# Moving three pieces of work in a four-layer decoder trunk: the bias-table copies, the first memory loads, and the rotary query product

## The chip, the core and the metric

The kernel runs on one core of a Trainium2 chip. The metric is the device time of one execution in microseconds (us), the median over the runs shown. One more execution was taken with the hardware profiler, and all rows of the profile come from that one.

## The reference, cut to what matters

There are 256 rows of 2048 features, four layers and one memory of 256 rows that every layer attends to.

```python
mem_n = rmsnorm(mem, mem_norm)
for i in range(4):
    h = rmsnorm(x, norm_in[i])
    # kinds 0, 1, 2, 0: latent attention, sparse attention, window attention, latent attention
    self_out, mq, gate = branch[i % 3](h, w_in[i], ...)
    mem_out = memory_attention(mq, mem_n @ w_mem_kv[i])     # 4 heads of 256, softmax over the memory
    y = concat([self_out, mem_out]) * silu(gate)            # 2048 + 1024 features
    x = x + y @ w_out[i]
out = rmsnorm(x, final_norm)
```

- Latent attention (layers 0 and 3) projects h to a query vector of 1536, a key-value vector of 512 and one shared rotary key of 64. Each of its 16 heads then takes a query of 128 plain and 64 rotary features from the normalized 1536 (`w_uq`), and a key and a value of 128 from the normalized 512 (`w_ukv`).
- Sparse attention (layer 1) has 32 heads, 4 key heads, and 16 index heads: for each query it adds relu(index query · index key) over the 16 heads with weights, and only the 64 keys with the best sums count. A bias by distance and head is added to the logits.
- Window attention (layer 2) has the same heads, a window of 128, a sink for each head, and the same bias.

All is float32 at the input and the output.

## The kernel before, in words

**Products.** Each float32 operand is split into a high and a low part (`split`, L62: a copy on ScalarE makes the high part, a subtraction on VectorE the low one), and each product is made of high×high, high×low and low×high. `rows_by` (L212) puts 128 rows of x on the output partitions: for each tile of 128 features it makes 3 products for each of the two row tiles (L227 to L229), as wide as the columns asked for, 512 at most. `columns_by` (L232) puts the output columns on the partitions (L246, 512 wide, and L250, 256 wide). Weights come by `stage` (L190) through SyncE's DMA queue into `wr`, a ring of 5 buffers of 4 KB a partition; `parts_of` splits a tile of them into `wh` and `wl`, rings of 3. The sums stand in PSUM tiles `acc`, 4 in all. Smaller products and transposes use 4 PSUM tiles `mp`.

**Buffers by name.** `PQ` = 5 buffers hold queries and keys (`qn`, `kn`, `qS`, `mkr`, `mqT`), `AUX` = 3 hold values and the like (`va`, `qrT`, `vs`, `mvr`). A pool hands out its buffers in the order in which the code asks for them. `big0` to `big3` hold what lives through a layer: in layers 1 and 2 first `iqT` (the index queries) and then `vz` (the split values) in `big1` and `big2`. The ring `e` of 4 holds softmax rows, and in `select` the relu'd scores `rl`.

**Order.** A scheduler with a timeline model of the engines puts the instructions of each engine into one fixed queue when the kernel is built; what is wrapped in `tc.keep_in_program_order` keeps its place in its engine's queue. On the chip each queue runs in that order, and an instruction that has to wait holds all behind it.

**Stages.** `memory()` (L305) first makes the keys and values of the memory for all four layers, from `w_mem_kv`, and stores them to DRAM (`mkT`, `mv`) by GpSimd's DMA queue. The same loop makes two small bias tables (`bias_table`, 32×384), and spreads them by `table_copies` (L130) over 128 rows: 8 DMAs of 1.5 MB from DRAM to DRAM, one in each of its 8 steps, but two in step 1 and none in step 7.

Each layer then runs `first()`. For latent attention that is the "small projection" of 576 columns in two products of 288 (`kva`, `kvb`), which gives the key-value vector and the rotary key `kr`, and then 1536 columns `cq`. For the others it is `kv`, giving the doubled keys `kd` (`mixer.k`), then in layer 1 `select()`: index products `iq`, then for each block of 128 queries 16 small products `isp` (L745), each followed by a relu on ScalarE (`rl`, L748) and a weighted sum on VectorE (`sco`, L753), and then 8 rounds of MAX8 and MATCH_REPLACE8 on VectorE (L760, L761). After that, `vz` is zeroed by two memsets on GpSimd (L689) and filled.

Then come six parts in the order 4, 0, 1, 2, 3, 5: parts 4 and 5 are halves of the memory attention (`memory_project`, `memory_attend`), the others groups of self heads (`project`, `attend`). The output product `w_out` (L827) of a part runs after the next part's attention: 4 chunks of 512 columns, each added to x (L832).

`memory_project` (L476) asks for two value buffers `mvr` and a key buffer `mkr` for each of its two heads, and loads them by GpSimd's DMA queue; between, it makes the memory queries (`acc_mq`) and drains each into `mqT` by `head_parts` (L260: ScalarE copies, VectorE `zl` L265 and `mqT` L266). The scores `msp` (L502) need `mkr`.

`Latent.project` (L605) makes for its group of four heads first the rotary queries (`acc_qr`, `rows_by`, 256 columns, 12 feature tiles), turns and transposes them, then the plain queries `qn`, the keys `kn`, the values `va` and the gate.

Of the kernel before, what the change touches and what calls it, by code (L numbers as in the profile page):

```python
# [8 lines left out]
F32 = mybir.dt.float32  # L9
# [6 lines left out]
P = 128  # L16
S = 256
# [7 lines left out]
MEMW = 1024  # L25
ST = 2
N_TAB = 384
PQ, AUX, WR = 5, 3, 5


@with_exitstack
def kernel(ctx: ExitStack, tc: tile.TileContext, a: dict, out: bass.AP,
# [97 lines left out]
    def table_copies(v, g):  # L130
        src = bass.AP(tensor=flat[v].tensor, offset=flat[v].offset + g * 8 * N_TAB,
                      ap=[[0, P], [1, 8 * N_TAB]])
        tc.keep_in_program_order(nc.gpsimd.dma_start(tabs[v][g].rearrange("p h n -> p (h n)"), src))


    def rsqrt_mean(dst, ssq, n):
# [168 lines left out]
    def memory():  # L305
        mrstd = cst.tile([P, 2], F32, name="mrstd")
        m16 = cst.tile([P, 2], F32, name="m16")
        mbc = act.tile([P, S], F32, name="mbc", tag="kr", bufs=1)
        mss = small("mss", 8, bufs=2)
        mT = [act.tile([P, 2, 4, S], F32R, name="mT", tag=f"big{c}") for c in range(4)]  # L310

        def prepare(c):
            if c < 3:
                mft.append(features(a["l_mem"], c + 1))
            if c == 1:
                tc.keep_in_program_order(nc.sync.dma_start(ident, a["c_ident"]))
                nc.vector.tensor_copy(identr, ident)
            weighted_parts(mT[c], mft[c], c * 4)

        def memory_rows(c):  # L320
            q = act.tile([P, 2, 512], F32, name="mrow", tag="pq", bufs=PQ)
            for t in range(2):
                tc.keep_in_program_order(
                    nc.sync.dma_start(q[:, t, :], min_[t][:, c * 512:(c + 1) * 512]))
            return q

        def row_scales(mrow):
            for c in range(4):
                for t in range(2):
                    square_sum(mss[:, t * 4 + c:t * 4 + c + 1], mrow[c][:, t, :])  # L330
            s2 = small("ms2", 2)
            nc.vector.tensor_reduce(s2, mss.rearrange("p (t c) -> p t c", t=2), AX.X, OP.add)
            rsqrt_mean(mrstd, s2, D)
            nc.vector.tensor_scalar(m16, mrstd, 0.0625, None, op0=OP.mult)
            spread(mbc, m16)

        def values(i, p_, acc):
            v = [act.tile([P, 2, 512], F32R, name="mv", tag="aux", bufs=AUX) for z in range(2)]
            for t in range(2):
                sc = mrstd[:, t:t + 1]  # L340
                copy_act(v[0][:, t, :], acc[t], scale=sc)
                nc.vector.scalar_tensor_tensor(v[1][:, t, :], acc[t], sc, f32(v[0])[:, t, :],
                                               op0=OP.mult, op1=OP.subtract)
            for z in range(2):
                nc.gpsimd.dma_start(mv[i][p_][:, z], v[z])

        def keys(i, h, acc):
            kT = act.tile([P, 2, 2, S], F32R, name="mkT", tag="pq", bufs=PQ)
            for j in range(2):
                z = total(acc[j])  # L350
                zs = wk.tile([P, S], F32, name="zs", tag="z", bufs=3)
                nc.vector.tensor_mul(zs, z, mbc)
                split(kT[:, 0, j, :], kT[:, 1, j, :], zs)
            nc.gpsimd.dma_start(mkT[i][h], kT)

        copies = [(v, g) for v in range(2) for g in range(4)]
        for i in range(depth):
            w = a["w_mem_kv"][i]
            for p_ in range(2):

                begins = i == p_ == 0
                acc = rows_by(mT, 16, w, 0, (MEMW + p_ * 512, 512), "mv", prepare if begins else None)
                if begins:
                    mrow = [memory_rows(c) for c in range(4)]
                else:
                    values(i, p_, acc)
                for h in (2 * p_, 2 * p_ + 1):
                    acck = columns_by(mT, 16, w, 0, (h * 256, 256), "mk")
                    if begins and h == 0:
                        row_scales(mrow)  # L370
                        values(i, p_, acc)
                    keys(i, h, acck)
                if begins:
                    late_constants()
                step = 2 * i + p_
                if step == 0:
                    bias_table(0)
                    bias_table(1)
                if 2 <= step < 6:
                    first_rows(step - 2)  # L380
                    nm.chunk(step - 2)
                if step == 6:
                    nm.finish()
                for c in copies[:2 if step == 1 else 1]:
                    table_copies(*c)
                copies = copies[2 if step == 1 else 1:]


    def transposed(dst, srcs):
# [83 lines left out]
        return weights_T(es, [(0, 0), (1, 0), (1, 1)])  # L473


    def memory_project(nm, i, w, mq0, g0, part):  # L476
        kT, qT = [], []
        v = [act.tile([P, 2, 512], F32R, name="mvr", tag="aux", bufs=AUX) for z in range(2)]
        for z in range(2):
            nc.gpsimd.dma_start(v[z], mv[i][part][:, z])  # L480
        for h in range(2):
            k = act.tile([P, 2, 2, S], F32R, name="mkr", tag="pq", bufs=PQ)
            nc.gpsimd.dma_start(k, mkT[i][2 * part + h])
            kT.append(k)
            acc = columns_by(nm.at, 16, w, 0, (mq0 + part * 512 + h * 256, 256), "mq")
            q = act.tile([P, 2, 2, S], F32R, name="mqT", tag="pq", bufs=PQ)
            head_parts(q, acc)
            qT.append(q)
        return nm, kT, v, qT, gate(nm, w, g0 + 2048 + part * 512)
# [49 lines left out]
    class Latent:  # L539
# [6 lines left out]
        def first(self):  # L546
# [55 lines left out]
            for z, sg in zip(self.scale, (1.0, -1.0)):  # L602
                nc.vector.tensor_scalar(z, qr, sg * (A_NOPE + A_ROPE) ** -0.5, None, op0=OP.mult)

        def project(self, g):  # L605

            j = self.j
            wq, wkv = a["w_uq"][j], a["w_ukv"][j]
            qn, kn = [], []
            qr = act.tile([P, 4, S], F32R, name="qrT", tag="aux", bufs=AUX)  # L610
            v = act.tile([P, 2, 512], F32, name="va", tag="aux", bufs=AUX)
            acc = rows_by(self.cT[:3], 12, wq, 0, (g * 768, 4, 192, A_NOPE, A_ROPE), "qr")
            for t in range(2):
                rr = wk.tile([P, 4, A_ROPE], F32, name="qrr", tag="z", bufs=3)
                rope(rr, acc[t][:, :S].rearrange("p (h d) -> p h d", h=4), t, 4)
                rs = wk.tile([P, 4, 2, A_ROPE], F32R, name="qrs", tag="qrs", bufs=1)
                split(rs[:, :, 0, :], rs[:, :, 1, :], rr)
                transposed(lambda i0, i1: qr[:, i0:i1, t * P:(t + 1) * P],
                           [rs[:, h].rearrange("p a b -> p (a b)") for h in range(4)])
            for half in range(2):  # L620
                acc = columns_by(self.cT[:3], 12, wq, 0, (g * 768 + half * 384, 2, 192, 0, A_NOPE), "qn")
                q = act.tile([P, 2, 2, S], F32R, name="qn", tag="pq", bufs=PQ)
                head_parts(q, acc)
                qn.append(q)
            for half in range(2):
                acc = columns_by(self.cT[3:], 4, wkv, 0, (g * 1024 + half * 512, 2, 256, 0, A_NOPE), "kn")
                k = act.tile([P, 2, 2, S], F32R, name="kn", tag="pq", bufs=PQ)
                head_parts(k, acc)
                kn.append(k)
            acc = rows_by(self.cT[3:], 4, wkv, 0, (g * 1024, 4, 256, A_NOPE, A_NOPE), "va")  # L630
            for t in range(2):
                copy_act(v[:, t, :], acc[t])
            return qn, qr, kn, v, gate(self.nm, self.w, self.g0 + g * 512)

        def attend(self, qn, qr, kn, v, gT):
            y = act.tile([P, 2, 4, S], F32R, name="y", tag="y", bufs=2)
# [180 lines left out]

    nm = Norm(0)
    memory()

    for i in range(depth):
        kind = kinds[i]
# [4 lines left out]
        def w_out(part, y, last):  # L827
            for c in range(4):
                acc = rows_by([y], 4, a["w_out"][i], part * 4, (c * 512, 512), "wo")
                for t in range(2):  # L830
                    xs = x[t][:, c * 512:(c + 1) * 512]
                    nc.vector.tensor_add(xs, xs, acc[t])  # L832
                if last and nxt is not None:
                    nxt.chunk(c)
                if last and nxt is None:
# [8 lines left out]
        order = [4, 0, 1, 2, 3, 5]  # L844
        for n_, part in enumerate(order):
            if part >= 4:
                y = memory_attend(*memory_project(nm, i, mixer.w, mixer.mq0, mixer.g0, part - 4))
            else:
                y = mixer.attend(*mixer.project(part))
            if pending is not None:  # L850
                w_out(*pending, False)
            pending = (part, y)
# [86 lines left out]
```

## Time and profile before

| | us |
|---|---|
| runs | 2639.67, 2634.15, 2635.05 |
| median | 2635.05 |
| profiled execution, its own time | 2636.8 |
| span of the profiled execution | 2634.7 |
| TensorE busy in the span | 2601.2 (99%) |
| VectorE / ScalarE / GpSimd busy | 1884.1 / 1628.8 / 57.3 |

The span runs from the first to the last instruction in the trace. Busy times of the engines overlap. In rows of instructions the columns are: start in us, time in us, engine, source line, operation, output and inputs, their sizes, how many were merged into the row, and in brackets how long the engine had been idle before it and what ended that. Products on TensorE are pipelined: the time from the start of one to the start of the next is what one costs, and it is shorter than the time in its own row. In tables by stretch there stand start and end, the length, then for each engine its busy time and in brackets its instructions, then the granted TensorE clock (`PEclk`, 1.00 is full), the busy share of the DMA engines, and GB/s.

### The profile page before, as it was taken

How to read it: one execution, taken by the hardware profiler on the slowest of the kernel's cores; microseconds unless marked ns; L12 is line 12 of the kernel's file. 1: busy time of each engine (PE TensorE's matmuls, PEld its weight loads, DVE VectorE, ACT ScalarE, POOL GpSimd, SP SyncE). 2: the span in 40 equal slices, each digit the busy share in tenths (PEclk: the TensorE clock that was granted, in tenths of full speed). 3: DMA queues.
4: the chain of work that ended last, by engine and by line, in shares of the span. 5: the costliest groups of instructions: out<-in, count | busy, mean ns of one | idle time of the engine just before them, and what ended most of it. 6: DMA issues, size and time to landing. Idle time of an engine off the chain costs nothing.

```text
span 2634.7 us, 42943 instructions
## 1 busy us (share of the span) xinstructions
PE 2601.2 (99%) x14556; PEld 2254.7 (86%) x14556; DVE 1884.1 (72%) x4171; ACT 1628.8 (62%) x3476; POOL 57.3 (2%) x101
## 2 busy tenths in 40 slices
PE   8999999999999999999999999999999999999998
PEld 7888888888888889888888888888888888888886
DVE  6566656677767685877777776777778767776767
ACT  6455556556656566666666666676666655665655
POOL 1000000000000000000000000000000000000000
PEclk9999999999999999999999999999999999999999
DMA  9889886666557665555555555555555666655764
GB/s 305 279 287 300 281 256 198 166 185 168 169 160 224 192 192 172 167 183 170 173 163 191 188 190 177 173 172 178 189 168 162 205 165 186 165 170 156 226 183 135
DMA packets 456924, 511.70 MB, mean 194 GB/s; under 512 B 69584, under 2 KB 352480, under 8 KB 455552
## 3 DMA queue, kind: packets, MB, share of 16 engines
q1 hardware_dynamic: 443328, 451.75, 56.5%
q0 software_dynamic: 13088, 56.16, 6.6%
q8 instruction: 114, 1.87, 0.3%
q14 instruction: 106, 0.87, 0.1%
q10 hardware_dynamic: 288, 1.05, 0.1%
HBM read 489.91 MB, written 31.56 MB: 198 GB/s over the span
## 4 chain that ended last, share of the span: by engine, by line
PE 97%; DMA 1%; DVE 1%; ACT 0%; issue 0%; SPq 0%; ACTq 0%
PE acc_g L246 14%; PE acc_g L250 7%; PE acc_wo L227 7%; PE acc_wo L228 7%; PE acc_wo L229 7%; PE acc_mq L246 5%; PE acc_mk L246 5%; PE acc_qn L246 3%; PE acc_cq L246 3%; PE acc_mq L250 2%; PE acc_mk L250 2%; PE acc_q L227 2%; PE acc_q L228 2%; PE acc_q L229 2%; PE acc_mv L227 2%; PE acc_mv L228 2%
## 5 line engine op out<-in xcount | busy, mean ns | idle before, releaser
L64 DVE TENSOR_TENSOR wl<-wr,wh 128x512 fp32r<-128x512 f32 (+2 forms) x1776 | 1173.8, 664 | 645.1 <-ACT wh L60 614.2
L60 ACT ACTIVATE wh<-wr 128x512 fp32r<-128x512 f32 (+2 forms) x1776 | 1079.0, 609 | 837.3 <-PE acc_g L246 183.7
L246 PE MATMUL acc_g<-xT,wh 128*128 128x512 f32 x1536 | 489.0, 397 | 0.6 <-DVE z L257 0.6
L250 PEld LDWEIGHTS acc_g<-xT,wl 128*128 128x128 f32 x1536 | 285.2, 188 | 60.7
L250 PE MATMUL acc_g<-xT,wl 128*128 128x256 f32 x1536 | 311.0, 280 | 0.0
L228 PE MATMUL acc_wo<-wl,y 128*128 128x512 f32 x768 | 302.6, 394 | 0.6 <-DVE wl L64 0.5
L229 PE MATMUL acc_wo<-wh,y 128*128 128x512 f32 x768 | 299.1, 390 | 0.0
L246 PEld LDWEIGHTS acc_g<-xT,wh 128*128 128x128 f32 x1536 | 238.1, 189 | 4.8 <-issue 1.1
L227 PE MATMUL acc_wo<-wh,y 128*128 128x512 f32 x768 | 240.4, 393 | 0.7 <-ACT wh L60 0.6
L228 PEld LDWEIGHTS acc_wo<-wl,y 128*128 128x128 f32 x768 | 144.3, 188 | 30.0 <-DVE wl L64 1.4
L229 PEld LDWEIGHTS acc_wo<-wh,y 128*128 128x128 f32 x768 | 144.2, 188 | 28.4
L227 PEld LDWEIGHTS acc_wo<-wh,y 128*128 128x128 f32 x768 | 141.3, 188 | 27.8 <-ACT wh L60 1.0
L246 PE MATMUL acc_mk<-mT,wh 128*128 128x512 f32 x512 | 161.9, 398 | 2.4 <-ACT wh L60 2.4
L246 PE MATMUL acc_mq<-xT,wh 128*128 128x512 f32 x512 | 161.7, 397 | 0.0
L832 DVE TENSOR_TENSOR x<-x,acc_wo 128x512 f32<-128x512 f32 x192 | 125.7, 683 | 7.1 <-PE acc_wo L229 6.8
L246 PE MATMUL acc_qn<-cT,wh 128*128 128x512 f32 x384 | 123.2, 399 | 0.0
L246 PE MATMUL acc_cq<-xT,wh 128*128 128x512 f32 x384 | 120.8, 396 | 0.0
L250 PEld LDWEIGHTS acc_mk<-mT,wl 128*128 128x128 f32 x512 | 96.7, 189 | 23.4 <-DVE wl L64 0.8
L250 PEld LDWEIGHTS acc_mq<-xT,wl 128*128 128x128 f32 x512 | 93.7, 188 | 20.0
L250 PE MATMUL acc_mq<-xT,wl 128*128 128x256 f32 x512 | 102.5, 281 | 0.0
L228 PE MATMUL acc_q<-wl,xT 128*128 128x512 f32 x256 | 102.4, 400 | 0.0
L250 PE MATMUL acc_mk<-mT,wl 128*128 128x256 f32 x512 | 101.7, 280 | 0.0
(280 smaller groups left out, 4438.0 us busy)
## 6 DMA issues: line engine op xcount, KB each, us to landing
wr<-in_w_out_dram SPq DMA_DIRECT2D x192, 512.0 KB, 3.7
wr<-in_w_in_a_dram SPq DMA_DIRECT2D x176, 512.0 KB, 4.1
wr<-in_w_mem_kv_dram SPq DMA_DIRECT2D x128, 512.0 KB, 5.6
wr<-in_w_in_b_dram SPq DMA_DIRECT2D x112, 512.0 KB, 3.5
wr<-in_w_in_c_dram SPq DMA_DIRECT2D x104, 512.0 KB, 3.5
wr<-in_w_uq_dram SPq DMA_DIRECT2D x288, 128.0 KB, 2.6
tab<-flat POOLq DMA_DIRECT2D x8, 1536.0 KB, 11.1
wr<-in_w_in_a_dram SPq DMA_DIRECT2D x32, 288.0 KB, 3.0
```

The lines of the kernel that those rows point to most:

```text
L60: nc.scalar.activation(o, i, AF.Copy, scale=scale)
L64: nc.vector.tensor_sub(lo, src, f32(hi))
L227: nc.tensor.matmul(acc[t][:, :n], xh, wh[:, :n], start=first, stop=False)
L228: nc.tensor.matmul(acc[t][:, :n], xh, wl[:, :n], start=False, stop=False)
L229: nc.tensor.matmul(acc[t][:, :n], xl, wh[:, :n], start=False, stop=last)
L246: nc.tensor.matmul(acc[j], wh[:, o:o + P], q[:, :, kt % 4, :], start=kt == 0, stop=False)
L250: nc.tensor.matmul(acc[j][:, 0, :], wl[:, o:o + P], q[:, 0, kt % 4, :], start=False, stop=kt == kts - 1)
L832: nc.vector.tensor_add(xs, xs, acc[t])
```

## The change

- `table_copies` leaves `memory()`. Each call of `w_out` now starts one table copy, after its first chunk has been added to x, until all eight are issued: six in layer 0 and two in layer 1. `not_before` is what ties it: a copy of one column by GpSimd, which waits for that column and so holds what stands behind it in GpSimd's queue.
- In `memory_project` of part 4, `not_before` waits for the first column of `mixer.k` (or of `kr` in latent layers), and the loads of `mvr` and `mkr` for that part keep their program order behind it.
- The rotary queries of two groups are made by one product of 512 columns, once for groups 0 and 1 and once for 2 and 3, in `project` of the even group, after the values and ahead of the gate. Two buffers `qrT` hold the result.
- `AUX` is 5, and GpSimd's DMA descriptor area is 8192 bytes a partition.

```diff
-PQ, AUX, WR = 5, 3, 5
+PQ, AUX, WR = 5, 5, 5
...
+    def not_before(col):
+        tc.keep_in_program_order(nc.gpsimd.tensor_copy(small("tick", 1), col))
...
-        copies = [(v, g) for v in range(2) for g in range(4)]
...
-                for c in copies[:2 if step == 1 else 1]:
-                    table_copies(*c)
-                copies = copies[2 if step == 1 else 1:]
...
-    def memory_project(nm, i, w, mq0, g0, part):
+    def memory_project(nm, i, w, mq0, g0, part, behind):
         kT, qT = [], []
+        if part == 0:
+            not_before(behind)
         v = [act.tile([P, 2, 512], F32R, name="mvr", tag="aux", bufs=AUX) for z in range(2)]
+        pin = tc.keep_in_program_order if part == 0 else lambda inst: inst
         for z in range(2):
-            nc.gpsimd.dma_start(v[z], mv[i][part][:, z])
+            pin(nc.gpsimd.dma_start(v[z], mv[i][part][:, z]))
         for h in range(2):
             k = act.tile([P, 2, 2, S], F32R, name="mkr", tag="pq", bufs=PQ)
-            nc.gpsimd.dma_start(k, mkT[i][2 * part + h])
+            pin(nc.gpsimd.dma_start(k, mkT[i][2 * part + h]))
...
+        def rotary(self, g):
+            self.qr = [act.tile([P, 4, S], F32R, name="qrT", tag="aux", bufs=AUX) for z in range(2)]
+            acc = rows_by(self.cT[:3], 12, a["w_uq"][self.j], 0, (g * 768, 8, 192, A_NOPE, A_ROPE), "qr")
+            for t in range(2):
+                for z in range(2):
+                    rr = wk.tile([P, 4, A_ROPE], F32, name="qrr", tag="z", bufs=3)
+                    rope(rr, acc[t][:, z * S:(z + 1) * S].rearrange("p (h d) -> p h d", h=4), t, 4)
+                    rs = wk.tile([P, 4, 2, A_ROPE], F32R, name="qrs", tag="qrs", bufs=1)
+                    split(rs[:, :, 0, :], rs[:, :, 1, :], rr)
+                    transposed(lambda i0, i1: self.qr[z][:, i0:i1, t * P:(t + 1) * P],
+                               [rs[:, h].rearrange("p a b -> p (a b)") for h in range(4)])
...
         def project(self, g):
...
-            qr = act.tile([P, 4, S], F32R, name="qrT", tag="aux", bufs=AUX)
...
-            acc = rows_by(self.cT[:3], 12, wq, 0, (g * 768, 4, 192, A_NOPE, A_ROPE), "qr")
...
-            return qn, qr, kn, v, gate(self.nm, self.w, self.g0 + g * 512)
+            if g % 2 == 0:
+                self.rotary(g)
+            return qn, self.qr[g % 2], kn, v, gate(self.nm, self.w, self.g0 + g * 512)
...
     memory()
+    copies = [(v, g) for v in range(2) for g in range(4)]
...
                     nc.vector.tensor_add(xs, xs, acc[t])
+                if c == 0 and copies:
+                    not_before(xs[:, :1])
+                    table_copies(*copies.pop(0))
...
-                y = memory_attend(*memory_project(nm, i, mixer.w, mixer.mq0, mixer.g0, part - 4))
+                y = memory_attend(*memory_project(nm, i, mixer.w, mixer.mq0, mixer.g0, part - 4,
+                                                  f32(mixer.k[:, 0] if kind else mixer.kr)[:, 0, :1]))
...
-    nc = _bacc.Bacc("TRN2", target_bir_lowering=False, num_devices=1)
+    nc = _bacc.Bacc("TRN2", target_bir_lowering=False, num_devices=1,
+                     dynamic_dma_scratch_size=8192)
```

More of the change, by code (lines that the diff above doesn't have):

```diff
@@ L609, in project @@
             qn, kn = [], []
-            qr = act.tile([P, 4, S], F32R, name="qrT", tag="aux", bufs=AUX)
             v = act.tile([P, 2, 512], F32, name="va", tag="aux", bufs=AUX)
-            acc = rows_by(self.cT[:3], 12, wq, 0, (g * 768, 4, 192, A_NOPE, A_ROPE), "qr")
[L613 to L619, printed above, removed]
             for half in range(2):
```

## The prediction

> **What bounds the kernel now.** I read the page first, then the stretches of 66 us, then who ended the waits inside the bad stretches.
>
> ```profile
> span 2634.7 us, 42943 instructions
> PE 2601.2 (99%) x14556; PEld 2254.7 (86%) x14556; DVE 1884.1 (72%) x4171; ACT 1628.8 (62%) x3476; POOL 57.3 (2%) x101
> PE 97%; DMA 1%; DVE 1%; ACT 0%; issue 0%; SPq 0%; ACTq 0%
> ```
>
> TensorE (PE) is the bound: 33.5 us of the span are not its busy time, and the chain that ended last is 97% PE. So a change pays only by taking products off PE, by closing PE's gaps, or by avoiding the half clock that follows them. It costs as soon as it makes PE wait anywhere.
>
> ```profile
> 66.00:132.00 66.00, 63.56 (x308) 53.23 (x307) 37.30 (x63) 32.82 (x57) 4.50 (x9) 0.97 0.86 279
> 264.00:330.00 66.00, 64.74 (x340) 54.60 (x339) 42.00 (x86) 36.34 (x69) 3.37 (x7) 1.00 0.87 281
> 330.00:396.00 66.00, 62.89 (x357) 55.85 (x356) 38.84 (x76) 34.59 (x70) 5.31 (x10) 0.98 0.81 254
> 127.00:131.00 4.00, 4.00 (x15) 3.42 (x15) 3.17 (x6) 2.15 (x4) 1.09 (x2) 0.57 1.06 345
> 393.00:397.20 4.20, 4.20 (x22) 4.20 (x21) 1.56 (x4) 1.37 (x4) 0.00 (x0) 0.59 0.55 150
> ```
>
> The first number after the length is PE's busy time. Idle are 66 − 63.56 = 2.44, 1.26 and 3.11 us, 6.81 together. Behind the first and the last of them PE runs at a granted clock of 0.57 over 4 us and 0.59 over 4.2 us, which loses (1 − 0.57) × 4 = 1.72 and (1 − 0.59) × 4.2 = 1.72 us, 3.44 together. The three gaps thus cost 10.25 us. What ended them:
>
> ```profile
> 107.69 1.06 POOL L133 DMA_DIRECT2D tab<-flat  x2
> 125.70 1.15 ACT L60 ACTIVATE wh<-wr 128x512 fp32r<-128x512 f32 x2 [5.17 <-DMA wr<-in_w_mem_kv_dram]
> ...
> 289.66 0.53 POOL L133 DMA_DIRECT2D tab<-flat  x1
> 291.29 1.71 ACT L60 ACTIVATE xT<-ft,gvec 128x256 fp32r<-128x256 f32 x4 [2.33 <-DMA ft<-in_l_x_dram]
> ...
> 379.88 1.08 POOL L480 DMA_DIRECT2D mvr<-mv  x2
> 380.93 0.56 POOL L483 DMA_DIRECT2D mkr<-mkT  x1
> 391.43 1.27 ACT L60 ACTIVATE wh<-wr 128x288 fp32r<-128x288 f32 x3 [3.52 <-DMA wr<-in_w_in_a_dram]
> ```
>
> Each time ScalarE waited for a load that shared the DMA engines with GpSimd's traffic: two table copies at once, one copy beside the loads of x, and the first memory loads beside the weights of the small projection, whose tiles are short (288 columns). The change moves exactly these.
>
> **Edit 1, copies out of the memory stage: −5.4 us** (2.44 + 1.72 + 1.26). In the changed kernel nothing of GpSimd's but stores of keys and values is left there. The bounds are −5.4 and, if stores and weights collide alone, −4.2 (the single-copy gap stays). I take −5.4.
>
> What the copies cost at their new place is read from single copies in the memory stage, which ask for weights at the same pace:
>
> ```profile
> 336.00:347.50 11.50, 11.50 (x54) 9.56 (x53) 5.88 (x9) 5.24 (x9) 0.50 (x1) 1.00 0.95 310
> tab<-flat POOLq DMA_DIRECT2D x8, 1536.0 KB, 11.1
> ```
>
> The row spans one copy: the DMA engines are 95% busy, and PE has no idle time. The five `wr` buffers ahead hide it. Each new copy is alone in its `w_out`, so 8 × 0. The bounds are 0 and 1.26 each, as in the one single copy that met other loads. The column copies that release them take GpSimd alone, and the next add to that column of x comes one whole part later.
>
> **Edit 3, rotary queries: −3.8 us, and +1.5 behind it.**
>
> ```profile
> L227 PE MATMUL acc_qr<-wh,cT x192: 277/283/368, 519.6 to 2444.7; 128*128 128x256 f32 x192
> 520.27 0.40 PE L227 MATMUL acc_qr<-wh,cT 128*128 128x256 f32 x2
> 520.99 0.40 PE L227 MATMUL acc_qr<-wh,cT 128*128 128x256 f32 x2
> 560.28 0.62 PE L227 MATMUL acc_va<-wh,cT 128*128 128x512 f32 x2
> 561.64 0.62 PE L227 MATMUL acc_va<-wh,cT 128*128 128x512 f32 x2
> L64 DVE TENSOR_TENSOR wl<-wr,wh 128x512 fp32r<-128x512 f32 (+2 forms) x1776 | 1173.8, 664 | 645.1 <-ACT wh L60 614.2
> 641.00:648.00 7.00, 7.00 (x43) 6.17 (x42) 6.80 (x17) 3.92 (x9) 0.00 (x0) 1.00 0.61 161
> ```
>
> Six narrow products take 520.99 − 520.27 = 0.72, 0.12 each; six wide ones 561.64 − 560.28 = 1.36, 0.227 each. The 3 × 192 = 576 narrow ones become 288 wide: 288 × (0.24 − 0.227) = 3.8 us. The columns are the same; only the fixed part of each product goes. Turns and transposes stay as many and run beside the gate. But the attention of the group before, which ran beside `qr`, now ends beside the keys `kn`, where VectorE (third busy time in the last row) is already busy for 6.80 of 7.00 us. Two operations of a split's size (0.66 each, the mean in the row of L64) more there make up to 1.3 us a group, 8 groups; rings of 3 and four `acc` tiles hide most of it. I take 0.2 a group, 1.5 in all; bounds 0 and 10.6. If that cover is gone, it is rival 3 below.
>
> **Edit 2, first loads held, in layers 0 and 3: −4.8 us** (3.11 + 1.72). The key `kr` is there soon after `kvb`, and the memory scores come a whole `cq` and two `mq` later. What is late next would be `cq`'s weights, of full-size tiles; bounds −4.8 and 0.
>
> **Edit 2 in layer 1: +14.1 us.** Here the hold is not until the small projection is done. In the order in which GpSimd's queue is built, the two memsets of `vz` come first, then the column copy, `mvr` twice, `mkr` twice. The second memset waits for the last `isp` of `select`, as the index queries are in its buffer. And since pools hand out buffers in the order asked, `mqT` can't be given before `mkr` is. In the built order ScalarE's four `mqT` copies therefore stand behind 14 of the 16 `rl` of the second block, and VectorE's drains of them behind 12 or 13 of its 16 sums. All 4 `acc` tiles stay held by the two `mq` products, and PE's queue has the 16 `isp` pairs of the second block in a row, nothing between, then the gate. In the kernel before, the drains ran at 1082.47 and the gate's products stood between the `isp`.
>
> ```profile
> 1078.46 1.71 DVE L753 SCALAR_TENSOR_TENSOR sco<-rl,iw,sco 128x128 f32<-128x128 f32 x4
> 1082.47 0.74 DVE L265 TENSOR_TENSOR zl<-acc_mq,mqT 128x256 f32<-128x256 f32 x2
> 1086.34 0.29 DVE L760 MAX8 m<-sco 128x8 f32<-128x128 f32 x1
> 1087.05 0.29 DVE L760 MAX8 m<-sco 128x8 f32<-128x128 f32 x1
> 1101.84 1.00 DVE L753 SCALAR_TENSOR_TENSOR sco<-rl,iw,sco 128x256 f32<-128x256 f32 x2
> 1106.24 0.75 DVE L64 TENSOR_TENSOR vz<-vs,vz 128x256 fp32r<-128x256 f32 x2
> 1082.62 0.63 PE L246 MATMUL acc_g<-xT,wh 128*128 128x512 f32 x2
> 1083.32 0.62 PE L246 MATMUL acc_g<-xT,wh 128*128 128x512 f32 x2
> 1082.00 1.24 ACT L748 ACTIVATE rl<-isp 128x256 f32<-128x256 f32 x4
> 1105.07 1.07 POOL L689 MEMSET vz<- 128x1152 f32 x1 [16.90 <-ACT rl L748]
> ```
>
> The last line's bracket is not what I use; its length is. Zero is the first row, the last four sums of the first block; PE issues that block's last `isp` at about 0.5.
> - VectorE: four sums 1.7, two splits at 0.66, then 8 rounds at 1087.05 − 1086.34 = 0.71, 5.7, with a mask before and a selection after them, taken at the 0.29 of MAX8, which is as wide: 9.3. Then 16 sums at 1.00 / 2 = 0.5.
> - `rl` has 4 buffers and `isp` 4 PSUM tiles, so the last `isp` can't start before the 8th sum is done, 9.3 + 4 = 13.3, and one relu (1.24 / 4 = 0.3) after it: it ends at 14.0. From 0.5 on PE has 13 `mq` products (6 wide, 7 narrow, 2.2 us) and 32 `isp`, narrow ones too (3.8 us), to do. Idle: 13.5 − 6.0 = 7.5.
> - The gate's first product waits for the first `mqT` drain: 12 sums (9.3 + 6 = 15.3), two `zl` 0.7, one sum 0.5, two `vz` 0.75 (the memset ended at 14.0 + 1.07 = 15.1), one `zl` and one `mqT`, as wide, 0.75: 18.0. Idle: 4.0.
> - Then 24 gate products stand before the first `msp`: four take 1083.32 − 1082.62 = 0.70, so 4.2, to 22.2. `mkr` is issued after the memset at 15.1, the column copy and two `mvr`:
>
> ```profile
> 954.55 1.06 POOL L480 DMA_DIRECT2D mvr<-mv  x2 [61.66 <-PE mo L523]
> mkr<-mkT POOLq DMA_DIRECT2D x1, 512.0 KB, 8.5
> ```
>
> at about 16.3, and the one issued behind two `mvr` landed 8.5 us later: 24.8. Idle: 2.6. The sum is 14.1. A half clock behind these pauses (1.72, as above) falls mostly into the wait for `mkr`, which it makes no longer. Bounds: 11.5, if `mkr` is there at once, and 17.5 with two half-clock stretches that nothing hides.
>
> [...]
>
> **Edit 2 in layer 2: 0.**
>
> ```profile
> 1559.25 0.37 PE L395 MATMUL tr<-identr,hl 128*128 128x128 f32 x3
> 1570.89 0.64 PE L502 MATMUL msp<-mkr,mqT 128*128 128x256 f32 x4
> ```
>
> The transposes of the first keys end at 1559.6; a copy, the column copy and two `mvr` later `mkr` is issued at some 1561.7, and with 8.5 us lands at 1570.2, just before the 1570.89 at which `msp` wants it. The memsets there wait for the layer before only. Bounds 0 and 1.5.
>
> **Sum.** −5.4 − 4.8 + 14.1 + 0 − 3.8 + 1.5 = +1.6, on the profiled execution's 2636.8: 2638.4. That execution is 1.75 above the median of the runs, 2635.05, so the forecast is 2636.6. A measurement of this kernel tells about 0.2% (5.3 us) from no change, and this is within it: the gaps closed in one place open in another. Own range 2630 to 2643, from the bounds of layer 1 and half of those of edit 3.
>
> **Rivals.**
> 1. *The hold in layer 1 costs nothing* (my reading of its queues is wrong, or VectorE is through earlier). For it: before, PE shows no gap there. Against it: the order is fixed, and each wait has a row. Then 2636.6 − 14.1 = 2622.5. Chance 0.14.
> 2. *The copies starve `w_out`.* A copy of 1536 KB in 11.1 us takes 142 of the 310 GB/s in the row at 336.00, and weights at 512 KB for 12 wide products (2.72 us) ask for 193. That leaves 168, and less where a store of 512 KB runs too, so they fall behind by some 0.3 to 0.8 MB in each copy, against 2.6 MB in the ring; it decides from where the ring is not full when the copy starts. Price 8 × 1.26 = 10: 2646.7. Against it: the row without idle time. Chance 0.12. [...]
> 3. *VectorE bounds the keys* (edit 3 at its upper end): +10.6 instead of +1.5, so 2645.7. Chance 0.12.
> 4. That the change does not do what it says is part of the forecast: in layer 1 the hold is longer than its name.
>
> **How the numbers follow.** The forecast has 0.62, with 0.42 within 0.2%, 0.14 slower and 0.06 faster, as layer 1's term is open upwards. Rival 1 gives 0.13 faster and 0.01 same, rivals 2 and 3 together 0.22 slower and 0.02 same. In sum faster 0.19, same 0.45, slower 0.36. The range 2625 to 2648 takes in rivals 2 and 3 and leaves rival 1 and combinations outside.
>
> **What would show it.** Right: no idle PE and PEclk 1.00 from 66 to 396 us; PE waits of some 7, 4 and 3 us in layer 1, ended by ScalarE's `rl`, VectorE's `mqT` and the DMA of `mkr`; 288 wide `acc_qr`; no wait of `wh` for `wr` during a copy in `w_out`. Wrong: no PE gap near 1070 to 1090 us (rival 1), ScalarE waiting for `wr` in `w_out` (rival 2), PE waiting for VectorE at `kn` or `va` (rival 3), or a gap left at `kvb`.

## The result, and the profile after

The changed kernel takes 2641.1 us in the median of 12 runs (2638.26 to 2645.83), the kernel before 2635.2 us in as many runs beside it (2631.72 to 2639.67). The ratio is 1.0024, with a 95% interval from 1.0015 to 1.0032: slower by 5.9 us, where 2636.6 was forecast, 1.5 us more than before. That lies in the forecast's range of 2625 to 2648 and just beyond the 0.2% that it called no change.

The page of the changed kernel: span, busy times and the chain that ended last.

```profile
span 2638.5 us, 42111 instructions
...
PE 2598.8 (98%) x14268; PEld 2239.8 (85%) x14268; DVE 1878.1 (71%) x4123; ACT 1625.8 (62%) x3428; POOL 61.8 (2%) x113
...
PE 96%; DMA 1%; DVE 1%; ACT 1%; issue 0%; SPq 0%; DVEq 0%; ACTq 0%
```

TensorE is busy 2.4 us less, with 288 products less, and idle 39.7 us where it was 33.5. Stretches of 66 us show where (length, then busy time of PE, PEld, DVE, ACT, POOL, the granted clock, the DMA share, GB/s):

```profile
66.00:132.00 66.00, 66.00 (x334) 56.01 (x333) 39.70 (x65) 35.16 (x61) 3.23 (x6) 1.00 0.79 248
132.00:198.00 66.00, 64.88 (x331) 54.05 (x330) 41.86 (x76) 37.75 (x76) 3.19 (x6) 1.00 0.77 252
198.00:264.00 66.00, 64.64 (x316) 53.24 (x315) 41.27 (x71) 38.01 (x71) 3.20 (x6) 1.00 0.77 249
264.00:330.00 66.00, 65.38 (x342) 55.37 (x341) 42.67 (x88) 37.15 (x71) 2.66 (x5) 1.00 0.80 254
330.00:396.00 66.00, 66.00 (x400) 59.75 (x399) 41.11 (x82) 37.01 (x75) 2.66 (x5) 1.00 0.72 215
1056.00:1122.00 66.00, 56.97 (x313) 49.70 (x312) 54.09 (x142) 34.68 (x83) 5.38 (x9) 0.90 0.55 168
```

The first and the fifth row had 2.44 and 3.11 us of idle PE and lost clock; both are clean. Rows two to four are not: 1.12 + 1.36 + 0.62 = 3.1 us idle, where before had 1.3 in all three. The last row is layer 1: 9.03 us idle, none before. Who was waited for (us in total, times, longest):

```profile
PE acc_mv L231 <- ACT wh L60: 11.8, 5, 8.7
PE isp L754 <- ACT rl L757: 5.6, 1, 5.6
PE acc_g L250 <- DVE mqT L270: 3.5, 1, 3.5
```

8.7 of the first row is the start of the kernel; the other four are the short waits of the memory stage. The second and third are the two waits forecast for layer 1. None is for `kvb`, `kn` or `va`.

### The profile page after: what moved, and what is told of

It is laid out like the page before. It is cut to its first block, busy times and chain, and to the rows that moved or that the text cites. A ratio compares the mean times of both kernels' runs of the same rounds, so it can differ in the third digit from the quotient of the medians.

```text
span 2638.5 us, 42111 instructions
## 1 busy us (share of the span) xinstructions
PE 2598.8 (98%) x14268; PEld 2239.8 (85%) x14268; DVE 1878.1 (71%) x4123; ACT 1625.8 (62%) x3428; POOL 61.8 (2%) x113
## 4 chain that ended last, share of the span: by engine, by line
PE 96%; DMA 1%; DVE 1%; ACT 1%; issue 0%; SPq 0%; DVEq 0%; ACTq 0%
PE acc_g L250 14%; PE acc_g L254 7%; PE acc_wo L232 7%; PE acc_wo L231 7%; PE acc_wo L233 7%; PE acc_mq L250 5%; PE acc_mk L250 4%; PE acc_cq L250 3%; PE acc_qn L250 3%; PE acc_mq L254 2%; PE acc_q L231 2%; PE acc_q L232 2%; PE acc_q L233 2%; PE acc_mk L254 2%; PE acc_mv L231 2%; PE acc_mv L232 2%
```

## The experiments

Twelve kernels ran, each against the kernel before on the same chip. First the parts one by one. `not_before` is the column copy on GpSimd.

**The copies alone (e2).** Before, with this:

```diff
-                for c in copies[:2 if step == 1 else 1]:
-                    table_copies(*c)
...
+                if c == 0 and copies:
+                    not_before(xs[:, :1])
+                    table_copies(*copies.pop(0))
```

> The kernel before with the table copies alone moved behind the output products. Forecast's theory (each of the three collisions of the memory stage goes and nothing takes its place): 5.4 us less, 2629.8 us. Rival, formed on the trace of the changed kernel (four short waits for the rows of x take the place of the collisions): about 1 to 2 us less, 2633.5, with TensorE waiting for ScalarE's weight parts four times between 150 and 292 us.

Measured: 2633.58 against 2635.74, ratio 0.9991 (0.9983 to 1.0). 2.2 us less in the medians, with an interval from 0 to 4.5 us that leaves the forecast's 5.4 out. The rival has the time right, but its four waits are not all there: the profiled execution, at 2631.23 one of the faster ones, shows 0.14, 0.61 and 0.79 us of idle PE in the three stretches from 132 to 330 us.

**The rotary product alone (e3).** Before, with `rotary(g)` for two groups and `AUX` at 5.

> The kernel before with the merged rotary products alone (and the five buffers of the aux ring that they need). Forecast's theory: 3.8 us off TensorE and 1.5 back behind it, 2.3 us less, 2632.7. Rival (VectorE bounds the keys where the attention of the group before now ends): 6.8 us more, 2641.9, with TensorE waiting for VectorE at the keys.

Measured: 2632.57 against 2635.74, ratio 0.9989 (0.9981 to 0.9998): 3.2 us less, with no wait for VectorE at the keys. This kernel still has the copies in the memory stage, and shows something else there, the stretch of the first pause and the 4 us behind it:

```profile
66.00:132.00 66.00, 63.92 (x317) 53.04 (x316) 37.96 (x63) 33.34 (x58) 4.31 (x8) 1.00 0.86 277
...
127.00:131.00 4.00, 4.00 (x25) 3.52 (x24) 3.29 (x6) 2.34 (x5) 1.09 (x2) 1.00 0.96 313
```

The pause behind the two copies is there with 2.08 us, but no half clock follows it. In the profiled execution of before the same 4 us had 0.57, and in that of e4 (next), where the pause is 1.9 us, the clock falls too: 0.61 over the same 4 us, and 0.97 over the stretch, as in before.

**The hold alone, in all layers (e4).** Before, with the new `memory_project`.

> The kernel before with the hold of the first memory loads alone, in all four layers. Forecast's theory: 14.1 more in layer 1, 4.8 less in layers 0 and 3, so 9.3 us more, 2644.3. Rival (the hold costs nothing in layer 1): 4.8 us less, 2630.2.

Measured: 2645.25 against 2635.74, ratio 1.0037 (1.0025 to 1.0049): 9.5 us more where 9.3 was expected. The rival falls.

**The changed kernel with the hold in the latent layers only (e1).**

```diff
-        if part == 0:
+        hold = part == 0 and kinds[i] == 0
+        if hold:
             not_before(behind)
...
-        pin = tc.keep_in_program_order if part == 0 else lambda inst: inst
+        pin = tc.keep_in_program_order if hold else lambda inst: inst
```

> The changed kernel, but the first memory loads are held (column copy and fixed order) only in the two latent layers, 0 and 3. Forecast's theory (in layer 1 the hold keeps the query tiles from being handed out, and so TensorE from the index products): the 13 to 14 us of layer 1 go, no idle TensorE between 1056 and 1122 us beyond the 1 us of before, 2627 us. Rival (the pauses of layer 1 come from the merged rotary products or the table copies, and the hold is only beside them): the time stays at 2640 and the pauses remain.

Measured: 2626.82 against 2635.74, ratio 0.9964 (0.9952 to 0.9976): 14.3 us below the changed kernel's median. Layer 1 and one stretch of the memory stage:

```profile
264.00:330.00 66.00, 64.89 (x339) 54.76 (x339) 42.08 (x87) 36.90 (x70) 2.67 (x5) 1.00 0.79 251
...
1056.00:1122.00 66.00, 66.00 (x388) 58.15 (x387) 58.97 (x157) 41.43 (x99) 2.13 (x2) 1.00 0.50 157
```

The pauses of layer 1 come from the hold in that layer; the short waits of the memory stage stay, so they have nothing to do with it. The last pause of that stage, 1.26 us before, is 1.11 us here (66 − 64.89), with no table copy near it.

**Order of the tiles or lateness of the keys (e5, e6).** e5 keeps the hold of layer 1 behind both memsets, but asks the ring for the query tiles first; e6 keeps the order and asks for the loads ahead of the selection, so that they wait for `kd` alone.

```diff
 e5, in memory_project
+        late = part == 0 and kinds[i] == 1
...
+        for h in range(2 if late else 0):
+            queries(h)
         if part == 0:
             not_before(behind)
...
 e6, in Grouped.first
             if self.sparse:
+                v, key = memory_loads(self.i, 0, f32(self.k[:, 0])[:, 0, :1])
+                self.loads = v, [key(0), key(1)]
                 self.select()
```

In e5 `queries(h)` makes the `mq` products of one head and drains them into `mqT`.

> The changed kernel with the hold kept as it is in layer 1 (behind both memsets of vz), but there the two memory query tiles are asked of their ring before the two key tiles. Forecast's theory (the order in which the ring hands out tiles is what stops TensorE, the late keys are only their last part): the waits for rl and mqT go, the scores of memory are reached behind the gate instead of within it, and the time is that of the kernel with the hold in the latent layers alone, 2627, or up to 2629.5 if the keys still land late. Rival (the late landing of the keys is the cost, and the order only shows it elsewhere): 7 to 14 us of waiting reappear at msp, 2634 to 2641.

> The changed kernel with the column copy and the four held loads of layer 1 put ahead of the selection, so that they are held until the key tile kd is written, and not behind the memsets of vz. Forecast's theory: the loads land while the index products run, their tiles are there before the query tiles are asked for, no pause in layer 1, 2627. Rival (2.1 MB of loads beside the weights of the index queries starve ScalarE there as they did in the memory stage): one or two pauses with a half clock, 3 to 10 us more, 2630 to 2637, with TensorE waiting at the products of iq.

Measured: e5 2625.38, ratio 0.996 (0.9948 to 0.9973); e6 2627.04, ratio 0.997 (0.9959 to 0.9981), both against 2635.34. Both are at e1's level. In e5 GpSimd's queue stands behind the second memset as in the changed kernel, and the keys are asked for even later, at 1097.57:

```profile
1095.26 1.07 POOL L705 MEMSET vz<- 128x1152 f32 x1 [16.90 <-ACT rl L764]
1096.27 0.29 POOL L137 COPY tick<-kd 128x1 f32<-128x1 f32 x1
...
1097.57 1.08 POOL L495 DMA_DIRECT2D mkr<-mkT  x2
```

The scores of memory, by tile (the two numbers behind the durations are the first and the last start), and the stretch:

```profile
L512 PE MATMUL msp<-mkr,mqT x24: 277/283/283, 1105.9 to 1118.8; 128*128 128x256 f32 x24
```

```profile
1056.00:1122.00 66.00, 66.00 (x387) 58.12 (x386) 58.78 (x157) 40.48 (x97) 5.51 (x9) 1.00 0.65 208
```

The keys wait for the memset, the scores start at 1105.9, and PE has no idle time: with the gate's products free to run there is work enough until then. So the 14 us need both: keys held until behind the second memset, and a ring that hands out the query tiles only after them. e5 changes the order alone and e6 the lateness alone, and either takes the cost away. In e6 the four loads issued from 999.59 on, beside the weights of the index queries, made no pause (12 us from 999, all busy):

```profile
999.00:1011.00 12.00, 12.00 (x61) 9.86 (x60) 5.80 (x11) 7.58 (x15) 3.39 (x7) 1.00 0.96 311
```

**The four short waits of the memory stage (e7, e8, e9).** In the changed kernel, ScalarE and then PE:

```profile
153.06 1.71 ACT L60 ACTIVATE xT<-ft,gvec 128x256 fp32r<-128x256 f32 x4 [2.17 <-DMA ft<-in_l_x_dram]
154.68 1.66 ACT L60 ACTIVATE wh<-wr 128x512 fp32r<-128x512 f32 x3
...
155.35 0.73 PE L231 MATMUL acc_mv<-wh,mT 128*128 128x512 f32 x2 [1.10 <-ACT wh L60]
```

The bracket of the first row is 2.17 us in which ScalarE stood for a feature tile of x, in order, with weight parts behind it. e7 asks for that tile ahead of the step's second keys; the first is issued at 139.5 us instead of 147.5, three weight loads earlier in SP's queue (its expectation says eleven):

```diff
                 for h in (2 * p_, 2 * p_ + 1):
+                    if h % 2 and 2 <= 2 * i + p_ < 6:
+                        ft = features(a["l_x"], 2 * i + p_ - 2)
```

> The kernel with the hold in the latent layers alone, and the loads of the four feature tiles of x asked for some eleven weight loads earlier, ahead of the second keys of their step. Theory formed on the trace (ScalarE, in order, waits for a feature tile that was asked for too late, and the weight parts behind it starve TensorE): no wait of xT for ft, the four short pauses of the memory stage go, 5 to 6 us less than the kernel with the hold in the latent layers alone, 2621. Rival (the DMA engines, at 0.77 of their time and stores of keys beside, are what is late, and the weights would be late in place of the rows): the pauses move to waits for weights, 2625 to 2628.

Measured: 2625.67 against 2635.34, ratio 0.9962 (0.9949 to 0.9974), 1 us from e1. The time is the rival's, but not its mechanism, and the row shows which wait it is:

```profile
144.32 0.91 ACT L60 ACTIVATE xT<-ft,gvec 128x256 fp32r<-128x256 f32 x2 [2.67 <-DMA ft<-in_l_x_dram]
```

The scheduler moved the reading forward with the load, and ScalarE stands there earlier and no shorter: 9.4 us in four waits, where e1 has 6.2 in four. So e8 ties the reading to the second keys of the step, and e9 ties the sums of squares of x's rows to the first ones, each by a column that is computed from the key tile times zero:

```diff
+            late = small("late", 4)
+            nc.vector.scalar_tensor_tensor(late, after, 0.0, gs, op0=OP.mult, op1=OP.add)
...
+            one = small("one", 1)
+            nc.vector.tensor_scalar(one, after, 0.0, 1.0, op0=OP.mult, op1=OP.add)
```

> The kernel with the hold in the latent layers alone, the feature tiles of x asked for some eleven weight loads earlier, and their reading by ScalarE tied to the second keys of the step, so that it stays at its old place in ScalarE's queue (moving the load alone had moved the reading too). Theory (ScalarE stands at xT for a tile that was asked for too late): no wait of xT for ft, the pauses at 155, 201, 246 and 292 us gone, some 3.5 us less than the kernel with the hold in the latent layers alone, 2623. Rival (the pauses come from the length of the four parts of xT in ScalarE's queue, 1.7 us, and not from the wait): the pauses stay, 2626.

> As the one before, and also the sums of squares of x's rows tied to the first keys of the step, since ScalarE waits up to 2.2 us for those rows as well. Theory: both kinds of waits go from ScalarE's queue, the memory stage shows no idle TensorE from 66 to 396 us, 0.5 to 1.5 us less than the one before, 2622. Rival (the waits for the rows of x are covered by the weight parts ahead): no change to the one before, 2623.

Measured against 2635.31: e8 2621.59, ratio 0.9945 (0.9931 to 0.9958); e9 2619.93, ratio 0.9936 (0.9924 to 0.9948). In e8 the reading stands at its old place and waits for nothing, and its stretches from 66 to 396 us have no idle PE. They have none in e9 either:

```profile
150.35 1.71 ACT L60 ACTIVATE xT<-ft,late 128x256 fp32r<-128x256 f32 x4
```

```profile
132.00:198.00 66.00, 66.00 (x342) 56.31 (x341) 45.32 (x88) 42.20 (x82) 3.20 (x6) 1.00 0.83 268
198.00:264.00 66.00, 66.00 (x333) 55.99 (x332) 42.03 (x73) 37.84 (x68) 3.20 (x6) 1.00 0.80 257
264.00:330.00 66.00, 66.00 (x344) 56.35 (x343) 45.59 (x99) 39.20 (x74) 3.20 (x6) 1.00 0.79 251
```

e9 is the best version, 21 us below the changed kernel and 15 below the one before. The difference of e8 and e9, 1.7 us, is inside both intervals, and as e8's stretches were full already, it is not shown that the tied squares brought anything.

**The copies, with those waits gone (e10, e11).** e10 is e9 with the copies back in the memory stage; e11 is e1 with a second copy of the same size behind each.

> As the one before, but with the table copies put back into the memory stage, where the kernel before has them. Theory (the forecast's term for the copies was right for the collisions alone, and the waits for the rows of x took part of it back): 5.4 us more than the one before, 2627.4. Rival (the copies cost there no more than the 2.2 us that moving them alone brought): 2624.2.

> The kernel with the hold in the latent layers alone, and behind each table copy a second one of the same size into a spare tensor that nothing reads: 16 copies of 1536 KB in place of 8, two in a row behind the same output product. Forecast's theory (the ring of weight tiles hides a copy in an output product at no cost): with two in a row still no wait of wh for wr, 2627. Rival (the ring is only just enough for one copy, so that a second starves TensorE): at each place the 2.4 us pause with or without the 1.7 us of half clock that two copies in a row made in the memory stage, so 8 x 2.4 to 8 x 4.1, 19 to 33 us more, 2646 to 2660.

Measured: e10 2620.18, ratio 0.9942 (0.993 to 0.9955), 0.25 us above e9 in the median: three of its five runs are at 2619.1 to 2620.2, two at 2623.0 and 2623.6. Theory and rival both asked for more in the median; the upper group is nearer to the rival's 2624.2. Its profile is of the run at 2623.0:

```profile
66.00:132.00 66.00, 63.97 (x310) 53.57 (x310) 37.49 (x63) 33.13 (x58) 4.30 (x8) 0.97 0.87 279
...
127.00:131.00 4.00, 4.00 (x17) 3.43 (x17) 2.46 (x5) 1.62 (x3) 1.09 (x2) 0.68 1.11 370
...
264.00:330.00 66.00, 66.00 (x347) 56.44 (x346) 45.19 (x95) 38.65 (x74) 3.18 (x6) 1.00 0.88 279
```

The two copies in a row still make a pause of 2.0 us. The lower group of runs is at e9's level (2618.6 to 2620.1), where a pause of 2.0 us would have to show; no profile tells whether it is there. The single copy beside the loads of x, to which I had put 1.26 us, makes none: the pause at 291 was the feature tile's, not the copy's.

e11 took 2637.88 against 2636.27, ratio 1.0009 (1.0 to 1.0018): 11 us above e1 in the medians, 10.5 when each is set against the kernel before beside it, and between the two expectations. PE waits behind four of the eight places for more than 0.5 us, and ScalarE for weights. Of the two lists of waits, PE's:

```profile
PE acc_q L234 <- ACT wh L60: 2.9, 2, 1.6
PE acc_mq L253 <- ACT wh L60: 2.7, 1, 2.7
...
PE acc_kv L234 <- ACT wh L60: 0.8, 1, 0.8
```

and ScalarE's:

```profile
ACT wh L60 <- DMA wr<-in_w_in_b_dram: 11.5, 5, 3.8
...
ACT wh L60 <- DMA wr<-in_w_in_a_dram: 4.7, 1, 4.7
```

The weight ring hid one copy behind an output product and not two, and the waits came in the stage that follows the output product, not in it.

**No hold at all (e12).** e9 with `hold = False`.

> The kernel with the squares of x tied to the first keys, and with no hold in any layer. Forecast's theory (the first memory loads collide with the weights of the small projection in layer 0): the pause of 3.1 us with a half clock is back at kvb, 4.8 us more than with the hold in the latent layers, 2624.7, and layer 3, where it showed no pause, unchanged. Rival (with nothing else in the queues the loads no longer collide): no pause at kvb, 2620.

Measured: 2623.98 against 2636.27, ratio 0.9953 (0.9941 to 0.9966), 4.05 us above e9 in the medians. The two ran on different chips; when each is set against the kernel before beside it, the difference is 3.1. The pause is back, with its half clock in the stretch:

```profile
330.00:396.00 66.00, 62.63 (x378) 57.07 (x377) 36.64 (x71) 34.49 (x70) 4.28 (x8) 0.97 0.74 231
```

```profile
PE acc_kvb L240 <- ACT wh L60: 3.4, 1, 3.4
```

## Why the forecast was off by 4.5 us, by its own steps

| step | forecast | measured alone |
|---|---|---|
| copies out of the memory stage, and their cost in `w_out` | −5.4, 0 | −2.2 (e2) |
| rotary product | −3.8 + 1.5 | −3.2 (e3) |
| hold, layers 0 and 3 | −4.8 | −4.05 (e12 against e9) |
| hold, layer 1 | +14.1 | +14.3 (changed kernel against e1) |
| sum | +1.6 | +4.9, and +5.9 in one |

Each of these differences has an interval of about 2 us to either side (e2: from 0 to 4.5), so 4.9 and 5.9 agree.

**The copies out of the memory stage: the step that failed.** The step said that three collisions cost 2.44 + 1.72 + 1.26 us and that nothing takes their place. Two of these three numbers were wrong for what they were used for.
- The 1.26 at 293: the row quoted for it had ScalarE waiting for `ft`, and I put that to the copy that was issued 1.6 us ahead. With the copies gone ScalarE's wait for `ft` came four times, as the row below shows, where before had it three times, 4.3 us; with the copies back and `ft` asked for earlier (e10) it came not at all. What is late is the tile, asked for behind the ring's weights. The table below shows when PE pauses for it: its pause is ScalarE's wait less some 1.07 us, so it takes a wait of more than that. What makes the wait longer or shorter, from 0.8 to 2.3 us, stays open; it is not the copies alone, as e3 and e4, which have them where before has them, show 1.83 and 2.42 us of idle PE in these stretches. That a pause at 126 lets the loads run ahead is only argued.
- The 1.72 of half clock behind the first pause: it was there in the profiled executions of before, e4 and e10, and not behind the same pause in e3. I took one execution's half clock as every execution's. e10's runs, in two groups 3 to 4 us apart, fit a cost that comes and goes, but only one of them has a profile. So how the missing 3.2 us divide between the two numbers stays open.

| us | ScalarE's waits for `ft`, in order | PE idle in 132 to 198, 198 to 264, 264 to 330 |
|---|---|---|
| before | none, 1.09, 0.93, 2.33 | 0, 0.02, 1.26 |
| changed | 2.17, 1.67, 1.83, 1.68 | 1.12, 1.36, 0.62 |
| e2 | 1.20, 1.68, 0.83, 1.85 | 0.14, 0.61, 0.79 |

The second and the third wait fall into the middle stretch: in the changed kernel 1.67 − 1.07 + 1.83 − 1.07 = 1.36. The waits of e3 and e4 fit in the same way.

ScalarE's wait in the changed kernel (us in total, times, longest):

```profile
ACT xT L60 <- DMA ft<-in_l_x_dram: 7.4, 4, 2.2
```

**The copies in `w_out`: right.** In the changed kernel and in e1 no output product waits for a weight part, but for two waits, of 0.6 and 0.5 us, that the kernel before has too. e11 gives the missing size of that cover: one more copy at each of the eight places costs some 11 us in all.

**The rotary product: the saving right, the cost behind it not there.** The changed kernel's wide products stand as forecast, six in 546.69 − 545.33 = 1.36 us:

```profile
545.33 0.62 PE L231 MATMUL acc_qr<-wh,cT 128*128 128x512 f32 x2
...
546.69 0.62 PE L231 MATMUL acc_qr<-wh,cT 128*128 128x512 f32 x2
```

No wait for VectorE shows at `kn` or `va`, so the 1.5 us should have been nothing, and rival 3 falls. e3 measured 3.2 against the 3.8 of the products alone, well inside its interval.

**The hold in layers 0 and 3: right**, 3.1 to 4.05 against 4.8. Layer 3, where no pause was seen, cannot be told apart from nothing. **Layer 2: right**; no pause there, PE is busy for 66.00 us from 1500 to 1566 and from 1566 to 1632.

**The hold in layer 1: right in its mechanism and its sum, and in two of its three places.** The stage in PE's and GpSimd's timelines, with one row of VectorE's:

```profile
1071.77 2.25 PE L754 MATMUL isp<-ikd,iqT 128*128 128x256 f32 x16
...
1079.20 6.37 DVE L762 SCALAR_TENSOR_TENSOR sco<-rl,iw,sco 128x256 f32<-128x256 f32 x11
...
1079.57 4.97 PE L754 MATMUL isp<-ikd,iqT 128*128 128x256 f32 x16 [5.55 <-ACT rl L757]
...
1084.66 1.06 POOL L698 MEMSET vz<- 128x1152 f32 x1 [9.47 <-PE isp L754]
1085.67 0.18 POOL L137 COPY tick<-kd 128x1 f32<-128x1 f32 x1
...
1086.86 1.07 POOL L486 DMA_DIRECT2D mkr<-mkT  x2
...
1088.02 0.79 PE L250 MATMUL acc_g<-xT,wh 128*128 128x512 f32 x1 [3.47 <-DVE mqT L270]
...
1093.89 1.59 PE L505 MATMUL msp<-mkr,mqT 128*128 128x256 f32 x12
```

The zero of the forecast's count, the last four sums of the first block, is at 1069.27 here. The last index product ends at 1084.54, 15.3 behind it (forecast 14.0); the gate starts at 18.75 (18.0); the scores of memory at 24.6 (24.8). The parts:
- The drip of the index products: 5.55 us idle, and the last sixteen take 4.97 us where the first took 2.25. That is 5.55 + 2.72 = 8.3 where 7.5 was forecast. A sum took 6.37 / 11 = 0.58 us and not the 0.5 of the forecast, and the products follow the sums.
- The wait for `mqT`: 3.47, forecast 4.0.
- The last 2.6 us were put to `mkr`. PE shows no wait for it: the 24 gate products take 1093.89 − 1088.02 = 5.9 us instead of 4.2, at a clock of 0.50 up to 1091.5, and by then the key is there: the two landed 6.4 and 7.2 us after their issue at 1086.9 and 1087.4, not 8.5, the first at 1093.3. The forecast had said that a half clock would fall into this wait; it took 1.7 of the 2.6 us, and of a wait for `mkr` nothing is left.

The three parts come to 8.3 + 3.5 + 1.7 = 13.5 us where 14.1 was forecast: one was too small and two too large, so part of the nearness of the sum is luck.

**The range.** The bounds that the forecast names for its own range, worked out, give 2632.5 to 2643.8 and not 2630 to 2643; 2641.1 lies in both. The wide range, 23 us, would have held a good deal else.

**Rivals.** 1 (the hold costs nothing in layer 1) falls by e1 and e4. 2 (copies starve `w_out`) falls for one copy and holds from two on. The profile shows how the two queues shared the engines: around the single copy of the kernel before (336.00 to 347.50 us) GpSimd's queue took 55.0% of the DMA engines' time, with 288 packets and 2.10 MB (7.3 KB a packet), and SyncE's 39.8%, with 1204 packets and 1.46 MB (1.2 KB a packet). So the weights came at 127 GB/s where 193 were asked for, and fell behind by about 0.8 MB, an estimate; the ring of 2.6 MB covered that, and PE had no idle time.

## What to carry to other kernels

A load that is only held back can still cost an engine that needs none of its data (here 14.3 us), if its tile comes from a ring whose later tiles that engine does need: read in which order the ring hands out tiles, and ask for the held ones last (e5) or early enough (e6). A pause that stands beside a transfer is not yet caused by it: look at which tile the waiting engine names, and whether it was asked for in time. And take a half clock behind a pause from more than one execution before it goes into a sum.

## What the runs showed of the hardware

The clock in layer 1 of the changed kernel, in four stretches:

```profile
1074.00:1079.00 5.00, 0.02 (x1) 0.00 (x0) 4.45 (x21) 0.72 (x2) 1.06 (x1) 0.89 0.15 54
1079.00:1088.00 9.00, 4.97 (x16) 4.01 (x16) 7.85 (x20) 5.49 (x16) 3.33 (x7) 0.50 0.11 28
1088.00:1091.50 3.50, 3.48 (x11) 3.00 (x12) 3.40 (x10) 0.00 (x0) 0.99 (x2) 0.50 0.98 318
1091.50:1096.00 4.50, 4.50 (x31) 4.11 (x30) 4.40 (x13) 1.90 (x3) 0.00 (x0) 1.00 1.09 377
```

PE stops at 1074.0; 0.89 over 5 us puts the fall near 1077.9 (0.94 from 1077 to 1078 us, 0.50 from 1078 on). Sixteen products that kept PE busy for 4.97 of 9 us left it at 0.50; they came in pairs, one pair for each sum of VectorE (0.58 us). The clock came back at 1091.5, 3.5 us after the first gate product, with PE busy for 3.48 of them, so only 1.75 us was lost behind the last pause. In the memory stage of before it was low for 3.4 us (0.51 over 127.05 to 130.50 us, 1.00 on both sides) and came back 4.1 us after PE's first product behind the pause, at 126.38.

A pause of 2.44 us was followed by a half clock in the kernel before, one of 2.03 in e10 (0.57 and 0.68 over 127 to 131 us) and one of 1.9 in e4 (0.61 over the same 4 us), while one of 2.08 us in e3 was not (1.00). Which pause of this length is followed by a half clock, no run here tells.
